# Residual add and RMS norm on one core: the fourth group's store issued between the second and third group's loads

## The chip, the core and the metric

The kernel runs on one core of a Trainium2 chip. The core has several engines with instruction streams of their own. Four matter here: VectorE (DVE in the profile) and ScalarE (ACT) compute, SyncE (SP) does nothing but issue transfers, and the DMA engines, 16 of them, move data between the chip's main memory (DRAM) and the on-chip buffers. TensorE has no work in this kernel and GpSimd (POOL) next to none.

The metric is the device time of one execution in microseconds (us). Before the change the median of three timed runs is 4016.13 us, the lowest 4003.17 and the highest 4017.06.

## The reference

```python
def setup_inputs():
    batch, seq, dim = 32, 2048, 2048
    # x, residual: (batch, seq, dim) float32; gamma: ones(dim); eps: 1e-6

def reference(x, residual, gamma, eps):
    z = x + residual
    rms = np.sqrt(np.mean(z ** 2, axis=-1, keepdims=True) + eps)
    return (z / rms * gamma).astype(np.float32)
```

There are 65,536 rows of 2048 float32 values. Each row is read twice (once from `x`, once from `residual`) and written once, so that 3 x 536.87 MB cross between DRAM and the core. No row needs anything of another row.

## The kernel before

**Tiles.** The rows are cut into 65 tiles, numbered 0 to 64. A full tile has 128 partitions with 8 rows each (8.39 MB per array); tile 0 has 3 rows per partition and tile 64 has 5. Tile `i` lives in buffer `z[i % 2]`: `x` is loaded there, `residual` is added in place, the normalized result is written over it, and the store reads it from there. So there are two tiles' worth of `z`. The residuals go to `r_area`, 9 rows per partition, in which the next tile's residual overwrites what the present tile's additions have already read.

**Groups.** Transfers of `x` into `z` and of results out of `z` are cut by partition into `Q = 4` groups: group `q` is the partitions `q, q+4, q+8, ...`, 32 of them, with all their rows (`group`, L145). One group's transfer of a full tile is 2.10 MB. A store of group `q` counts up the semaphore `s_out[q]`; a load of any group counts up `x_in`. The residual of a tile is one transfer of 8.39 MB.

**Compute.** `dve_turn` (L210) waits until all four groups of `x` and the residual are there, adds in three pieces, and then scales in two halves, each after ScalarE has given the root of the mean square; the last instruction counts up `done`. `act_turn` (L258) squares and sums each row, and in the middle of tile `i`, once the second of the three additions is through, it issues the load of the residual of tile `i + 1` on its own DMA queue (L161, q10 in the profile).

**Transfers by SP.** After a short beginning SP runs `sp_turn(sp, i)` (L177) for `i` = 1 to 63. All its transfers go to one queue (q1). Turn `i` stores the results of tile `i - 1` and loads `x` of tile `i + 1` into the buffer that these stores empty, group by group. SP works strictly in program order, so a wait in front of one transfer holds back everything behind it:

1. it waits for `done` of tile `i - 1` (L184);
2. it issues the stores of groups 0, 1 and 2 (L186);
3. for groups 0, 1 and 2 it waits until that group's store has landed (`s_out[q]`, L181) and issues the load of that group (L182, reported under L149);
4. it issues the store of group 3 (L189);
5. it waits until that store has landed and issues the load of group 3 (L190).

Then comes turn `i + 1`. Behind the turns, `sync_program` stores tile 63 in two halves and tile 64 in three pieces (L175).

In the profile the stores of the groups are `out_dram<-z` of L170, the loads of `x` are `z<-in_x_dram` of L149, and the residual is `r_area<-in_residual_dram` of L161.

Of the kernel before, what the change touches and what calls it, by code (L numbers as in the profile page):

```python
# [9 lines left out]
def kernel(  # L10
# [32 lines left out]
    Q = 4  # L43
# [16 lines left out]
    def rows(t, i):  # L60
        k = sizes[i]
        return t[starts[i] : starts[i] + P * k, :].rearrange("(p r) m -> p r m", r=k)
# [82 lines left out]
    def group(q):  # L145
        return slice(q, P, Q)

    def load_x(sp, i, q):
        sp.dma_start(out=z[i % 2][group(q), : sizes[i], :], in_=rows(x_f, i)[group(q)]).then_inc(  # L149
            ev["x_in"][i % 2], U  # L150
        )
# [17 lines left out]
    def store(sp, i, q):  # L169
        sp.dma_start(out=rows(o_f, i)[group(q)], in_=z[i % 2][group(q), : sizes[i], :]).then_inc(  # L170
            s_out[q], U
        )
# [4 lines left out]
    def sp_turn(sp, i):  # L177


        def load(q):  # L180
            sp.wait_ge(s_out[q], i * U)  # L181
            load_x(sp, i + 1, q)  # L182

        Turn(i).wait(sp, "done", -1)  # L184
        for q in range(Q - 1):
            store(sp, i - 1, q)  # L186
        for q in range(Q - 1):
            load(q)
        store(sp, i - 1, Q - 1)  # L189
        load(Q - 1)  # L190


    def add(v, i, a, b):
# [92 lines left out]
    def sync_program(sp):  # L286
        whole_x(sp, 0)
        load_r(sp, Turn(0))

        sp.wait_ge(tail_ev["add"], 1)  # L290
        for q in range(4):
            sp.dma_start(  # L292
                out=stage[32 * q : 32 * q + 1],
                in_=gamma.partition_broadcast(1).rearrange("p (a b) -> p a b", a=16),
            ).then_inc(g_in, U)
        load_r(sp, Turn(1))
        whole_x(sp, 1)
        for i in range(1, last):
            sp_turn(sp, i)
        (a0, b0), (a1, b1) = halves(last - 1)  # L300
        sp.wait_ge(half, 1)
        store_rows(sp, last - 1, a0, b0)
        Turn(last).wait(sp, "done", -1)
        store_rows(sp, last - 1, a1, b1)
        for k, (a, b) in enumerate(tail):
            sp.wait_ge(tail_ev["done"], k + 1)
            store_rows(sp, last, a, b)
# [94 lines left out]
```

## Time and profile before

| what | value |
|---|---|
| median of the timed runs | 4016.13 us |
| the profiled execution's own time | 3982.87 us |
| its span, first to last instruction | 3981.1 us |
| VectorE busy | 2300.7 us (58%) |
| ScalarE busy | 1059.7 us (27%) |
| read from DRAM / written | 1073.77 MB / 536.87 MB |
| share of the 16 DMA engines' time, queue of SP (q1) | 65.9% |
| the same, queue of ScalarE (q10) | 30.5% |

The profile is one execution. Its page gives sums over the whole span; the timeline gives single instructions with their starts; the view by windows gives, for any stretch of the span, each engine's busy time, the mean busy share of the DMA engines and the rate at which they moved data. That view books a DMA packet whole to the moment at which it starts (a packet here is 64 KB on one of the 16 engines), so a short window can show a share over 1, and windows are best cut where a transfer begins. The start of an SP row is when SP issues a transfer; when the transfer has landed is seen from the instruction that waited for it.

### The profile page before, as it was taken

To read this page: it belongs to the slowest core of one execution; us is meant where nothing else is said; L and a number is where in the kernel's file an instruction comes from. 1 tells how busy PE (TensorE), PEld (TensorE's weight loads), DVE (VectorE), ACT (ScalarE), POOL (GpSimd) and SP (SyncE) were. 2 spreads that over 40 slices of the span, in tenths; PEclk is the share of its full clock that TensorE was granted. 3 is DMA by queue.
4 is the path that set the end of the run, shared out by engine and by line. 5 is a ranking of instruction groups with operands and counts; after the bars stand their busy time and mean duration, and the time that the engine had idled before them with its cause. 6 is when DMAs were issued, how large, how long until landed. Compare 5 with 4: busy or idle time off the path is not lost.

```text
span 3981.1 us, 4005 instructions
## 1 busy us (share of the span) xinstructions
DVE 2300.7 (58%) x842; ACT 1059.7 (27%) x1157; POOL 0.2 (0%) x4
## 2 busy tenths in 40 slices
DVE  5646556465564655646556465564655646556465
ACT  2313223132231322313223132231322313223132
POOL 0000000000000000000000000000000000000000
DMA  9999999999999999999999999999999999999999
GB/s 421 411 392 420 399 402 410 390 415 396 400 411 400 411 400 408 403 400 412 400 409 402 400 411 400 400 411 400 413 398 411 411 400 411 400 400 410 390 421 379
DMA packets 34694, 1610.73 MB, mean 405 GB/s; under 512 B 9280, under 2 KB 9344, under 8 KB 9344
## 3 DMA queue, kind: packets, MB, share of 16 engines
q1 hardware_dynamic: 25616, 1085.34, 65.9%
q10 hardware_dynamic: 9072, 525.34, 30.5%
q14 instruction: 6, 0.05, 0.0%
HBM read 1073.77 MB, written 536.87 MB: 405 GB/s over the span
## 4 chain that ended last, share of the span: by engine, by line
DMA 94%; SPq 3%; DVE 1%; issue 1%; another core or an unknown queue 1%; ACT 0%; ACTq 0%; DVEq 0%
DMA out_dram<-z 93%; SPq L170 2%; SPq L149 1%; DVE z L200 1%; DVE z L195 1%; DMA z<-in_gamma_dram 0%; DMA z<-in_x_dram 0%; ACT sq_junk L246 0%; SPq L292 0%; DVE z L311 0%; ACT rms L256 0%; DVE rstd L219 0%; ACTq L161 0%; DVE tail_rstd L329 0%
## 5 line engine op out<-in xcount | busy, mean ns | idle before, releaser
L195 DVE TENSOR_TENSOR z<-z,r_area 128x8192 f32<-128x8192 f32 (+2 forms) x192 | 1104.8, 5809 | 1589.9 <-DMA z<-in_x_dram 1579.0
L246 ACT ACTIVATE sq_junk<-z 128x2048 f32<-128x2048 f32 x512 | 962.1, 1879 | 2891.2 <-DVE z L195 2880.9
L200 DVE SCALAR_TENSOR_TENSOR z<-z,rstd,gamma_tile 128x2048 f32<-128x2048 f32 x507 | 1156.5, 2343 | 4.5
L246 ACT ACTIVATION_READ_ACCUMULATOR sq_junk<-z 128x1 f32 x512 | 95.4, 186 | 0.0
L219 DVE RECIPROCAL rstd<-rms 128x4 f32<-128x4 f32 (+1 forms) x128 | 22.3, 174 | 58.2 <-ACT rms L256 58.2
L256 ACT ACTIVATE rms<-ssq,eps_tile 128x4 f32<-128x4 f32 (+1 forms) x128 | 38.0, 297 | 11.7
L200 DVE SCALAR_TENSOR_TENSOR z<-z,tail_rstd,gamma_tile 128x2048 f32<-128x2048 f32 x5 | 11.6, 2346 | 0.1
L313 DVE LOAD_MASK_SELECT gamma_tile<-z x1 | 0.0, 14 | 16.3 <-DMA z<-in_gamma_dram 16.3
L195 DVE TENSOR_TENSOR z<-z 128x2048 f32<-128x2048 f32 x3 | 6.7, 2284 | 0.0
L313 DVE STREAM_SHUFFLE gamma_tile<-z 128x2048 f32<-128x2048 f32 x1 | 2.3, 2290 | 0.0
L311 DVE MEMSET z<- 128x2048 f32 x1 | 1.8, 1765 | 0.4 <-issue 0.4
L246 ACT ACT_TABLE_LOAD x1 | 1.3, 1283 | 0.9 <-SPq L80 0.9
L256 ACT ACT_TABLE_LOAD x1 | 1.3, 1283 | 0.1
L256 ACT ACTIVATE tail_rms<-tail_ssq,eps_tile 128x2 f32<-128x2 f32 (+1 forms) x3 | 0.9, 295 | 0.1
L310 DVE MEMSET eps_tile<- 128x1 f32 x1 | 0.1, 59 | 1.0 <-SPq L80 1.0
L329 DVE RECIPROCAL tail_rstd<-tail_rms 128x2 f32<-128x2 f32 (+1 forms) x3 | 0.5, 158 | 0.0
L383 POOL MEMSET const-bfloat16-1.0<- 128x1 bf16 x1 | 0.1, 101 | 0.0
L383 POOL MEMSET const-uint8-127<- 128x1 uint8 x1 | 0.1, 101 | 0.0
L383 POOL MEMSET const-float32-0.0<- 128x1 f32 x1 | 0.1, 98 | 0.2 <-issue 0.2
L383 POOL MEMSET const-float32-1.0<- 128x1 f32 x1 | 0.1, 98 | 0.0
## 6 DMA issues: line engine op xcount, KB each, us to landing
out_dram<-z SPq DMA_DIRECT2D x2, 4096.0 KB, 20.9
z<-in_x_dram SPq DMA_DIRECT2D x4, 1280.0 KB
r_area<-in_residual_dram ACTq DMA_DIRECT2D x1, 5120.0 KB, 25.6
out_dram<-z SPq DMA_DIRECT2D x2, 2048.0 KB, 8.6
z<-in_x_dram SPq DMA_DIRECT2D x249
out_dram<-z SPq DMA_DIRECT2D x248, 20.6
z<-in_x_dram SPq DMA_DIRECT2D x1, 3072.0 KB
z<-in_residual_dram SPq DMA_DIRECT2D x1, 3072.0 KB, 17.2
```

What stands on the lines that cost most here:

```text
L149: sp.dma_start(out=z[i % 2][group(q), : sizes[i], :], in_=rows(x_f, i)[group(q)]).then_inc(ev["x_in"][i % 2], U)
L170: sp.dma_start(out=rows(o_f, i)[group(q)], in_=z[i % 2][group(q), : sizes[i], :]).then_inc(s_out[q], U)
L195: return v.tensor_add(out=s, in0=s, in1=res(i, a, b))
L200: ins = v.scalar_tensor_tensor(out=s, in0=s, scalar=rs[:, c + g - a : c + g - a + 1], in1=gamma_tile[:, :], op0=mult, op1=mult,)
L219: v.reciprocal(out=rstd[p][h][:, :n], in_=rms[p][h][:, :n]).then_inc(dve, U)
L246: s.activation(out=sq_junk[:, :], in_=src[:, g, :], func=Act.Square, accum_out=sq[:, c + g - a : c + g - a + 1],)
L256: return s.activation(out=rm, in_=sq, func=Act.Sqrt, bias=eps_tile[:, :], scale=inv_d)
L310: v.memset(eps_tile[:, :], float(eps))
L311: v.memset(stage, 0.0).then_inc(tail_ev["add"], 1)
L313: v.stream_shuffle(gamma_tile[:, :].rearrange("p (a b) -> p a b", a=16), stage, [0] * 32)
L329: v.reciprocal(out=tail_rstd[:, a:b], in_=tail_rms[:, a:b]).then_inc(dve, U)
L383: nc = _bacc.Bacc("TRN2", target_bir_lowering=False, num_devices=1)
```

## The change

Only the order of SP's instructions within a turn changes. The store of group 3 is issued after the loads of groups 0 and 1, and before the load of group 2, where it was issued after the load of group 2. Nothing is added or removed: a turn still has four stores and four loads with the same sizes, the same waits stand in front of the same transfers, and no instruction of VectorE or ScalarE is touched. `load(q)` is the inner function of `sp_turn` that waits for `s_out[q]` and issues the load.

```diff
         for q in range(Q - 1):
             store(sp, i - 1, q)
-        for q in range(Q - 1):
+        load(0)
+        load(1)
+        store(sp, i - 1, Q - 1)
+        for q in range(2, Q):
             load(q)
-        store(sp, i - 1, Q - 1)
-        load(Q - 1)
```

SP's stream of a turn with full tiles before the change (turn 2 of 63; L170 is a store, L149 a load, each of one group; in brackets the semaphore that it waits for):

```order
L170 DMA out_dram<-z 32x16384 [waits done1]
L170 DMA out_dram<-z 32x16384 x2
L149 DMA z<-in_x_dram 32x16384 [waits s_out0]
L149 DMA z<-in_x_dram 32x16384 [waits s_out1]
L149 DMA z<-in_x_dram 32x16384 [waits s_out2]
L170 DMA out_dram<-z 32x16384
L149 DMA z<-in_x_dram 32x16384 [waits s_out3]
```

The same turn after the change:

```order
L170 DMA out_dram<-z 32x16384 [waits done1]
L170 DMA out_dram<-z 32x16384 x2
L149 DMA z<-in_x_dram 32x16384 [waits s_out0]
L149 DMA z<-in_x_dram 32x16384 [waits s_out1]
L170 DMA out_dram<-z 32x16384
L149 DMA z<-in_x_dram 32x16384 [waits s_out2]
L149 DMA z<-in_x_dram 32x16384 [waits s_out3]
```

The last store, which waits for nothing, has moved up by one load; between it and the load that waits for its landing there now stands the load of group 2, where nothing stood before.

SP's stream at the last turn (63, whose loads are those of the shorter tile 64) and the first store behind it, before the change:

```order
L149 DMA z<-in_x_dram 32x10240 [waits s_out1]
L149 DMA z<-in_x_dram 32x10240 [waits s_out2]
L170 DMA out_dram<-z 32x16384
L149 DMA z<-in_x_dram 32x10240 [waits s_out3]
L175 DMA out_dram<-z 128x8192 [waits half]
```

And after it:

```order
L149 DMA z<-in_x_dram 32x10240 [waits s_out1]
L170 DMA out_dram<-z 32x16384
L149 DMA z<-in_x_dram 32x10240 [waits s_out2]
L149 DMA z<-in_x_dram 32x10240 [waits s_out3]
L175 DMA out_dram<-z 128x8192 [waits half]
```

The same move is made there; the stores of the end stand where they stood.

## The prediction

> **What bounds the kernel now.** I begin with the page: the span, the engines, and the DMA rows.
>
> ```profile
> span 3981.1 us, 4005 instructions
> DVE 2300.7 (58%) x842; ACT 1059.7 (27%) x1157; POOL 0.2 (0%) x4
> DMA  9999999999999999999999999999999999999999
> GB/s 421 411 392 420 399 402 410 390 415 396 400 411 400 411 400 408 403 400 412 400 409 402 400 411 400 400 411 400 413 398 411 411 400 411 400 400 410 390 421 379
> DMA packets 34694, 1610.73 MB, mean 405 GB/s; under 512 B 9280, under 2 KB 9344, under 8 KB 9344
> ```
>
> No compute engine is near its limit, and the DMA engines are over nine tenths busy in every slice: the transfers set the time. A slice of about 100 us hides what happens within a turn, though. So I ask who waits, first all engines, then SP's queue:
>
> ```profile
> DVE z L195 <- DMA z<-in_x_dram: 1579.0, 63, 26.1
> DVE z L195 <- DMA r_area<-in_residual_dram: 11.0, 1, 11.0
> ```
>
> ```profile
> SPq L149 <- DMA out_dram<-z: 3612.7, 252, 38.2
> ```
>
> VectorE waits some 25 us for `x` in each turn, so neither it nor ScalarE sets the pace; for the residual it waited once. SP spends nearly the whole span waiting for stores to land before it may load. Such a wait costs nothing while the DMA queues hold other work. Whether they do is seen in one turn from the middle, SP's rows (the three loads of L149 from narrow windows), with the residual's issue and VectorE's first addition and last scaling of a tile:
>
> ```profile
> 1964.23 0.47 SPq L149 DMA_DIRECT2D z<-in_x_dram  x1
> 1964.74 1.87 SPq L170 DMA_DIRECT2D out_dram<-z  x3
> 1973.06 8.69 DVE L195 TENSOR_TENSOR z<-z,r_area 128x8192 f32<-128x8192 f32 x1 [25.00 <-DMA z<-in_x_dram]
> 1977.79 0.51 SPq L149 DMA_DIRECT2D z<-in_x_dram  x1
> 1982.63 0.51 SPq L149 DMA_DIRECT2D z<-in_x_dram  x1
> 1987.65 0.47 SPq L149 DMA_DIRECT2D z<-in_x_dram  x1
> 1988.16 0.60 SPq L170 DMA_DIRECT2D out_dram<-z  x1
> 1988.40 0.34 ACTq L161 DMA_DIRECT2D r_area<-in_residual_dram  x1
> 2005.33 4.60 DVE L200 SCALAR_TENSOR_TENSOR z<-z,rstd,gamma_tile 128x2048 f32<-128x2048 f32 x2
> 2026.19 0.47 SPq L149 DMA_DIRECT2D z<-in_x_dram  x1
> ```
>
> I call the loads L0 to L3 and the stores S0 to S3, by group. The first row is L3 of a turn; behind it S0, S1, S2 of the next turn are issued at once. L0, L1 and L2 follow as S0, S1 and S2 land, 4.84 and 5.02 us apart. S3 and the residual go out at 1988.2 to 1988.4. Then SP stands still for 38 us until S3 has landed at 2026.19, and only then issues the next L3. The next stores, whose data VectorE had ready at 2005.33 + 4.60 = 2009.93, stand in SP's program behind that L3. So at 2026.19, with S3 landed, what else is in the queues? Windows over the DMA engines, cut at these points, say nothing:
>
> ```profile
> 1972.05:1986.55 14.50, 13.49 (x2) 4.70 (x5) 0.00 (x0) 1.00 1.00 434
> 1986.55:2025.45 38.90, 22.39 (x12) 11.81 (x14) 0.00 (x0) 1.00 1.00 431
> 2025.45:2027.40 1.95, 0.00 (x0) 0.00 (x0) 0.00 (x0) 1.00 0.00 0
> 2027.40:2034.05 6.65, 0.00 (x0) 0.00 (x0) 0.00 (x0) 1.00 1.06 345
> 1965.45:2027.40 61.95, 35.88 (x13) 16.51 (x18) 0.00 (x0) 1.00 0.97 406
> ```
>
> The last two numbers of a row are the DMA share and the rate. While S0 to S2 run (first row) and while L0 to L2, S3 and the residual run (second), the engines are full: 434 and 431 GB/s. Then the residual and S3 end together, both queues are **drained**, and for 1.95 us no packet starts. L3, alone behind the hole, moves its 2.10 MB in 6.65 us, where 2.10 MB at 434 GB/s take 4.83. The whole turn takes 61.95 us for 4 + 4 + 4 times 2.10 MB = 25.17 MB; at 434 GB/s that is 57.99. **The hole and the slow restart together cost 61.95 - 57.99 = 3.96 us a turn**; 1.95 of it is the hole, 2.0 the rest.
>
> **The change part by part.** No instruction, byte or wait is added or removed, and no VectorE or ScalarE row moves. Three things move on SP's queue.
>
> *S3 is issued earlier.* It goes out behind L1, at about the 1982.6 of the rows above instead of 1988.16, past L2 and its wait for S2. S3 itself waits for nothing, its data being finished long before. In the queue it takes the third place, behind L0 and L1, instead of the fourth.
>
> *L2 stays where it was in time.* It still waits for S2's landing (1987.65 above), and issuing S3 in front of it costs the 0.60 us of its row at a moment when SP waits anyway. Ahead of it S2, L0, L1 and S3 fill the queue, so SP is not late; were that cover gone, it would be 0.6 us a turn, 37 us in all.
>
> *L3's wait for S3 is now covered.* After S2's landing the queue of SP holds L0, L1, S3, L2 and ScalarE's holds the residual: the same 16.8 MB as before, but the last in SP's queue is now L2, not S3. When S3 lands, all of L2 (4.83 us at 434 GB/s) and whatever is left of the residual are still to be moved. The way from S3's end to L3's first packet showed as the 1.95 us hole. So L3 arrives at least 4.83 - 1.95 = 2.9 us before the engines run dry, and more if the residual has not ended. Right behind L3 SP issues the next S0 to S2 without a wait: the tile's `done` comes 2009.93 - 1973.06 = 36.87 us after its `x` has landed, and a turn is 58 at the least, so these stores have over 20 us to spare. The hole does not move elsewhere: during S0 to S2 the next load is issued as each one lands, with at least one more store in the queue, as the first window shows already.
>
> What is late next? Nothing up to the DMA rate itself. VectorE's chain of 36.87 us is far under 58. The residual is issued 1988.40 - 1973.06 = 15.34 us after the tile's `x` landed. Its time to land is the same in every turn that I asked for (spans 100 to 3900):
>
> ```profile
> DMA to landing us min/median/max: 37.7/37.9/38.6
> ```
>
> 15.34 + 37.9 = 53.2 us, inside 58.
>
> How often? The hole needs a turn that is drained. These are the first L3 of that kind, the last, and the windows on them, with the L3 of turn 1 ahead of them:
>
> ```profile
> 90.85 0.47 SPq L149 DMA_DIRECT2D z<-in_x_dram  x1
> 158.82 0.47 SPq L149 DMA_DIRECT2D z<-in_x_dram  x1
> 3941.19 0.47 SPq L149 DMA_DIRECT2D z<-in_x_dram  x1
> ```
>
> ```profile
> 158.50:160.00 1.50, 0.00 (x0) 0.00 (x0) 0.00 (x0) 1.00 0.00 0
> 3940.90:3942.40 1.50, 0.00 (x0) 0.00 (x0) 0.00 (x0) 1.00 0.00 0
> ```
>
> Turn 1 (90.85) lies in the warm-up, where the residual's load still runs (VectorE's single wait for it, 11.0 us). Turns 2 to 63 are 62, and (3941.19 - 158.82) / 61 = 62.0 us a turn confirms the count. The saving is 62 x 3.96 = 245.5 us. At the end nothing changes but the start: VectorE's work on tile 64 and the last stores hang on its `x` as before.
>
> **Sum.** 3982.87 (the profiled execution's own time) - 245.5 = 3737.4 us. The median of the runs shown lies 4016.13 - 3982.87 = 33.3 us above the profiled run, from a cause that the profile doesn't show; I leave that distance in: **3771 us**. As a cross-check, 1610.73 MB at 434 GB/s are 3711 us; the 26 us on top are the beginning, the end, and warm-up.
>
> The size that the trace doesn't show is L3's pace when it starts with the engines full. From one side, it runs as S0 to S2 do (4.83 us); from the other, its slowness (6.65) is its own and only the 1.95 us hole goes: 62 x 1.95 = 121 us. I take the first, since L0, also a load, follows S2 in the second window, where 431 GB/s leave no room for such a delay. Both ends are kept for the range.
>
> At this place the Trainium skill has a rule on the price: "DMA: Bandwidth & Descriptors", Anatomy of one DMA, gives each transfer about 2.0 us fixed (fitted on the other way of issuing, by GpSimd), mostly the confirmation of the last byte. By it the covered round trip would be worth 62 x 2.0 = 124 us and the time about 3892; the hole's 1.95 us agrees, while the 6.65 us of L3 speak for more.
>
> **The rivals.**
>
> *Only the hole goes.* As worked out: 3982.87 - 121 + 33.3 = 3895 us. For it: L3's slow part comes after the hole. Against: no other load shows it.
>
> *The engines can't hold 434 for long.* The fullest slice of the page has 421 GB/s. At that rate throughout, 1610.73 MB take 3826 us; with the 33.3 and a few us of beginning, 3861. Against: that slice contains the beginning of the kernel, and the 38.90 us stretch ran at 431 with reads and writes mixed. On this the skill's "HBM Reference", Specifications (TRN2), has a rule: a core streaming alone gets about 425 GB/s, bounded by its DMA engines. By it 1610.73 MB take 3790 us, with 33.3 and the beginning about 3826; the windows here show more, so far over stretches of 39 us.
>
> *The change doesn't do what it says: no change, 4016 us.* If the empty 1.95 us were not the drained queue but a pause that the engines take between a turn's end and L3 whatever lies behind, the turn would stay at 62. Against: the hole sits exactly on SP's round trip, and no packets are queued then.
>
> *Slower: the residual becomes the late one.* It enters at 15.34 us into the tile, with L0, L1, S3 and L2 in SP's queue. If the engines served it only behind these (4 x 4.83 = 19.3 us) and then shared with L3 and the next stores packet by packet (2 x 19.3 us), it would land 58 us after its issue, and VectorE would start a tile every 15.34 + 58 = 73.3 us: 62 x (73.3 - 62.0) = 701 us more, 4717. It decides as soon as the residual takes over 62.0 - 15.34 = 46.7 us to land. Against: it lands in 37.9 now with as many transfers queued ahead or beside it.
>
> **How the numbers follow.** Forecast (hole and slow restart gone) 0.69; rate below 434 GB/s 0.10; only the hole 0.08; no change 0.08; residual late 0.05. The prediction is the likeliest, 3771. Downwards the floor is the profiled run's 3737 without the 33.3; a little under it the range begins, 3730. Upwards it takes in the rate and the hole cases, 3900. That leaves out no change and slower, 0.13, and a little at the edges. A measurement of this kernel tells about 0.5% from no change, some 20 us; the first three cases are faster by far more: 0.87 faster, 0.08 within it, 0.05 slower.
>
> **What would show it.** After the change a turn's L3 should be issued several us before the DMA engines have finished L2 and the residual, no window of 1.5 us at L3 should be empty, a turn should take about 58.0 us between equal rows of SP, L0 to L2 should still follow the landings of S0 to S2, VectorE's wait for `x` should shrink by about 4 us a turn, and the mean rate should be near 431 GB/s. A hole elsewhere, VectorE waiting for the residual in most turns, or L3 taking over 6 us with full queues would make the prediction wrong.

## The result and the profile after

| | before | after |
|---|---|---|
| median of the timed runs, us | 4010.93 (4 runs, 4003.17 to 4017.06) | 3740.54 (4 runs, 3735.12 to 3749.47) |
| the profiled execution's own time, us | 3982.87 | 3735.12 |
| mean rate over the span, GB/s | 405 | 431 |

The ratio of after to before is 0.9329, with a 95% interval of 0.9302 to 0.9356. The sum made against the profiled execution had given 3737.4 us; the profiled run after has 3735.12. The forecast for the median, 3771, lies 30 us too high, and that is taken up below.

The page of the changed kernel, its span, DMA rows and queues (packets, MB, share of the 16 engines' span):

```profile
span 3733.3 us, 4005 instructions
...
DMA  9999999999999999999999999999999999999999
GB/s 415 436 428 437 437 428 436 428 436 428 435 431 435 433 434 431 436 431 434 436 429 437 435 432 434 433 433 433 433 433 432 433 428 436 428 437 433 430 433 392
DMA packets 34694, 1610.73 MB, mean 431 GB/s; under 512 B 9280, under 2 KB 9344, under 8 KB 9344
## 3 DMA queue, kind: packets, MB, share of 16 engines
q1 hardware_dynamic: 25616, 1085.34, 67.4%
q10 hardware_dynamic: 9072, 525.34, 32.6%
```

The two shares add up to 100.0%; before they were 65.9 + 30.5 = 96.4%. The page shows no idle time of the DMA engines any more, and all slices but the first and the last lie between 428 and 437 GB/s, where they had lain around 405.

SP's rows of one turn from the middle (the lines of the file have moved by one behind the change, so L196 is the former L195):

```profile
1954.02 0.47 SPq L149 DMA_DIRECT2D z<-in_x_dram  x1
1970.98 0.51 SPq L149 DMA_DIRECT2D z<-in_x_dram  x1
1975.83 0.51 SPq L149 DMA_DIRECT2D z<-in_x_dram  x1
1976.38 0.68 SPq L170 DMA_DIRECT2D out_dram<-z  x1
1980.69 0.47 SPq L149 DMA_DIRECT2D z<-in_x_dram  x1
2012.09 0.47 SPq L149 DMA_DIRECT2D z<-in_x_dram  x1
2024.36 8.69 DVE L196 TENSOR_TENSOR z<-z,r_area 128x8192 f32<-128x8192 f32 x1 [21.22 <-DMA z<-in_x_dram]
```

These are L3, then L0 and L1 behind the landings of S0 and S1, S3 at once behind L1, L2 behind S2's landing, and L3 of the next turn. From L3 to L3 it is 58.07 us, where it was 61.96. S3 lands by 2012.09, and L3, issued then, is through when VectorE starts at 2024.36, 12.27 us later. Its 2.10 MB take 4.83 us at 434 GB/s, so by this estimate the engines still had some 7 us of other work when it was issued. Two windows over this turn, the first inside the stretch of S0 to S2, the second the whole turn:

```profile
1960.00:1974.50 14.50, 8.23 (x1) 0.00 (x0) 0.00 (x0) 1.00 1.00 434
...
1954.00:2012.10 58.10, 35.88 (x13) 16.53 (x18) 0.00 (x0) 1.00 1.00 433
```

The stretch of stores runs at the 434 GB/s that it had before; now the whole turn does (433, share 1.00). VectorE's waits, over all turns:

```profile
DVE z L196 <- DMA z<-in_x_dram: 1308.7, 62, 22.4
...
DVE z L196 <- DMA r_area<-in_residual_dram: 33.3, 2, 17.1
```

VectorE waits for its input (1579.0 + 11.0) - (1308.7 + 33.3) = 248.0 us less. That is the whole gain of the span, 3981.1 - 3733.3 = 247.8 us.

The shares also say of what the gain consists. Before, the DMA engines were idle for 3.6% of 3981.1 us, that is 143 us, and busy for 3838; now they are busy for all 3733 with the same bytes. So 143 us were idle time, 2.3 us for each of the 62 turns, and the other 105 us, 1.7 a turn, were packets that took longer.

### The profile page after: what moved, and what is told of

Read it like the earlier page. It is cut to its first block, busy times and chain, and to the rows that moved or that the text cites. A ratio compares the mean times of both kernels' runs of the same rounds, so it can differ in the third digit from the quotient of the medians.

```text
span 3733.3 us, 4005 instructions
## 1 busy us (share of the span) xinstructions
DVE 2300.7 (62%) x842; ACT 1060.9 (28%) x1157; POOL 0.2 (0%) x4
## 4 chain that ended last, share of the span: by engine, by line
DMA 92%; SPq 4%; DVE 2%; issue 1%; another core or an unknown queue 1%; ACT 0%; ACTq 0%; DVEq 0%
DMA out_dram<-z 90%; SPq L170 3%; SPq L149 2%; DVE z L196 1%; DMA r_area<-in_residual_dram 1%; DVE z L201 1%; DMA z<-in_gamma_dram 0%; DMA z<-in_x_dram 0%; ACT sq_junk L247 0%; SPq L293 0%; DVE z L312 0%; ACT rms L257 0%; DVE rstd L220 0%; ACTq L161 0%
## 5 line engine op out<-in xcount | busy, mean ns | idle before, releaser
L196 DVE TENSOR_TENSOR z<-z,r_area 128x8192 f32<-128x8192 f32 (+2 forms) x192 | 1104.8, 5810 | 1342.0 <-DMA z<-in_x_dram 1308.7
L196 DVE TENSOR_TENSOR z<-z 128x2048 f32<-128x2048 f32 x3 | 6.7, 2284 | 0.0
## 6 DMA issues: line engine op xcount, KB each, us to landing
out_dram<-z SPq DMA_DIRECT2D x248, 21.5
```

What stands on the lines that cost most here:

```text
L196: return v.tensor_add(out=s, in0=s, in1=res(i, a, b))
```

## The experiments

The theory: the time came from the drained queues at each turn's end, and anything that stands in a queue while SP learns that S3 has landed removes it. The rivals: the early place of S3 or the mixing of stores and loads is what helps, or the hole alone (121 us) and not what the prediction calls the slow restart. Each experiment below ran beside the kernel before on the same chip; in the first four that has a median of 4002.39 us (19 runs), in the last four 4002.49 (9 runs). They are called e1 to e8 in the order in which they stand; the last section holds e7 and e8.

### The kernel before, again

No edit.

> The kernel before, once more, for its scatter: its profiled run lay 33 us under the median of its timed runs, while the changed kernel's profiled run lies 5 us under its median. Theory A (the distance sits in the hole at the end of each turn: the round trip from S3's landing to L3's first packet, and L3's restart, vary from run to run): about 4000 to 4017 us, and a profile of a slower run shows 62.0 plus up to 0.5 us a turn, with the difference in the hole or in L3, while the stretch with full queues still runs at 431 to 434 GB/s. Theory B (a difference between chips or runs that touches everything): the full-queue stretch itself is slower by 0.8%, about 427 to 430 GB/s.

Measured: 4003.65 us median of 10 runs, 3997.74 to 4008.96; ratio 0.9999 (0.9989 to 1.0008). Its profiled run was one of the slower ones. Its page, the queues, and windows over one turn (S0 to S2; L0 to L2, S3 and the residual; a stretch around L3's issue in which no packet starts; L3), and under them the like stretch in the first profile of this kernel:

```profile
span 4006.5 us, 4005 instructions
...
q1 hardware_dynamic: 25616, 1085.34, 65.5%
q10 hardware_dynamic: 9072, 525.34, 30.5%
```

```profile
1982.50:1997.00 14.50, 13.30 (x2) 4.51 (x5) 0.00 (x0) 1.00 1.00 434
1997.00:2035.70 38.70, 22.57 (x12) 11.99 (x14) 0.00 (x0) 1.00 1.00 434
2034.50:2038.30 3.80, 0.00 (x0) 0.00 (x0) 0.00 (x0) 1.00 0.00 0
2038.30:2045.00 6.70, 0.00 (x0) 0.00 (x0) 0.00 (x0) 1.00 1.00 313
```

```profile
2023.55:2027.35 3.80, 0.00 (x0) 0.00 (x0) 0.00 (x0) 1.00 0.00 0
```

The stretches with full queues are not slower, so theory B falls: S0 to S2 run at 434 GB/s in both profiles, and the second stretch moves the same 16.8 MB at a share of 1.00 (the prediction's 431 for it comes from a window that ends 0.2 us further in the stretch without starts). The engines were busy 96.0% of 4006.5 us, that is 3846 us, against 3838 in the first profile: of the 25.4 us more, about 17 are idle time and 8 longer packets (each share is rounded to 0.1%, 4 us). All 38 runs of this kernel in the experiments lie between 3996 and 4010 us, above the 3982.87 of the profile that the prediction was read from; why that one run was faster isn't shown. Theory A holds for most of the distance, but not by a longer hole: in both turns shown no packet starts for 3.80 us. The packet records of the two traces from 150 to 3650 us say where the idle time is. No engine has a packet for 1.6 us a turn in both, but an engine is idle for 2.4 us a turn on average in the first and 2.7 in the second, so in the second the engines run dry further apart from each other.

The same rows correct the reading of the hole. A packet takes 2.42 us where the queues are full (14.50 us for six of them on each engine), so of the 3.80 us without a start the first 2.4 are still covered by packets that run. The prediction's 1.95 us began 1.9 us into this stretch, and its start was chosen, not measured. L3 behind the hole has a share of 1.00 over 6.70 us for two packets on each engine: the engines are busy, with packets of 3.35 us.

### All four stores ahead of the loads

Against the changed kernel:

```diff
-        for q in range(Q - 1):
+        for q in range(Q):
             store(sp, i - 1, q)
-        load(0)
-        load(1)
-        store(sp, i - 1, Q - 1)
-        for q in range(2, Q):
+        for q in range(Q):
             load(q)
```

> All four stores of a turn ahead of its loads: S0 S1 S2 S3, then L0 to L3. Theory (only that something stands in the queue behind S3 when it lands): the same as the changed kernel, 3735 to 3750 us, no hole, about 58.1 us a turn; a better covered round trip brings nothing more. Rival (the place between the loads matters, since stores and loads mix better there): slower than the changed kernel by tens of us, 3770 or more, with the full-queue rate under 431 GB/s. Rival (the earlier the store, the better): faster than 3735.

Measured: 3732.47 us median of 4 runs (3732.05 to 3732.95), ratio 0.9318 (0.9303 to 0.9334), which overlaps with that of the changed kernel. The page's two queues add up to 99.9%. The place between the loads is not what helps: with no load between the stores it is as fast. The median lies just under the theory's 3735, where the last rival had put it. Whether this order is a little faster was left to a run of both on one chip, below.

### S3 where it was, L3 behind the next turn's S0

Against the kernel before:

```diff
-        def load(q):
+        def load(q, i=i):
...
         Turn(i).wait(sp, "done", -1)
-        for q in range(Q - 1):
+        store(sp, i - 1, 0)
+        if i > 1:
+            load(Q - 1, i - 1)
+        for q in range(1, Q - 1):
             store(sp, i - 1, q)
         for q in range(Q - 1):
             load(q)
         store(sp, i - 1, Q - 1)
-        load(Q - 1)
+        if i == last - 1:
+            load(Q - 1)
```

> S3 is left where it was before the change, behind L2; instead L3 and its wait for S3 are moved behind the first store S0 of the next turn, so that S0 stands in the queue when S3 lands. Theory (any cover does): no hole, 58 to 58.5 us a turn, 3740 to 3765 us; VectorE waits less for x since x lands about 5 us later. Rival (S3's early place is what brings the time): about 4010 us as before.

Measured: 3756.48 us median of 4 runs (3754.18 to 3757.49), ratio 0.9377 (0.9362 to 0.9393). S3 stands behind L2 as before the change, and 246 of the 4002.39 us go all the same. So it is not S3's early place; a store that covers the wait for S3 removes the holes as well. This is the clearest of the runs on that question, since it shares with the changed kernel nothing but the cover. The page's queues are full, as they are after the change:

```profile
q1 hardware_dynamic: 25616, 1085.34, 67.5%
q10 hardware_dynamic: 9072, 525.34, 32.4%
```

The span is 3754.8 us, 21.5 longer than that of the changed kernel, at 99.9% busy: that difference is mostly packets that took longer, and why is open.

### The changed order, and the drained queue put back

Against the changed kernel, a wait for the landing of L0 to L2 in front of L3:

```diff
-        for q in range(2, Q):
-            load(q)
+        load(2)
+        sp.wait_ge(ev["x_in"][(i + 1) % 2], ((i + 1) // 2) * Q * U + (Q - 1) * U)
+        load(3)
```

> The changed kernel with its order, and one wait more: SP issues L3 only when L0 to L2 have landed. S3 keeps its early place; only the emptied queue comes back. Theory (the hole is the cost): an empty window of about 2 us ahead of each L3, L3 in about 6.7 us, 62 us a turn, 3980 to 4010 us. Rival (the order brings the time, the empty queue does not matter): 3740 to 3760 us.

Measured: 4011.79 us median of 10 runs, ratio 1.0021 (1.0011 to 1.0031): the whole gain is gone, and 9 us more. Its L3, VectorE's start on that tile, and a window ahead of L3's first packet:

```profile
2035.27 0.47 SPq L149 DMA_DIRECT2D z<-in_x_dram  x1
2044.34 8.69 DVE L197 TENSOR_TENSOR z<-z,r_area 128x8192 f32<-128x8192 f32 x1 [26.05 <-DMA z<-in_x_dram]
```

```profile
2032.60:2036.40 3.80, 0.00 (x0) 0.00 (x0) 0.00 (x0) 1.00 0.00 0
```

The hole is back, again 3.80 us without a packet's start, and L3 takes 9.07 us from issue to VectorE's start, as the 8.91 us (2026.19 to 2035.10) did in the kernel before. With e3 this settles the point from both sides: without the order and with the cover the time is gained, with the order and without the cover it is lost.

### A hole between L3 and S0

Against the changed kernel, SP waits for all of `x` of the tile in work ahead of S0:

```diff
         Turn(i).wait(sp, "done", -1)
+        Turn(i).wait(sp, "x_in")
         for q in range(Q - 1):
```

> The changed kernel, and before S0 of each turn SP waits until all of x of the tile in work has landed (L3 is then the last transfer out, both queues are empty). The emptied queue now lies between L3 and S0 instead of between S3 and L3, so the first transfers behind it are three stores, issued together, in place of one load. Theory A (the cost is the round trip plus a slow restart of whatever comes first): a hole of about 2 us and a restart of about 2 us a turn, 62 us, 3980 to 4010 us. Theory B (the slow 6.65 us is peculiar to a load that runs alone with nothing behind it or to reads from DRAM): only the hole of about 2 us, 60 us a turn, 3855 to 3885 us. If neither hole nor slowness costs anything: 3740.

Measured: 3980.61 us median of 4 runs (3978.99 to 3982.72), ratio 0.9946 (0.9931 to 0.9962). In total it is theory A's number, though 22 us (0.5%) under the kernel before. One turn by windows: the hole; 12.15 us of stores; 3 us at the end of S2; the rest; 3 us from the middle of the rest; the next hole; the turn from hole to hole:

```profile
1970.60:1972.05 1.45, 0.69 (x1) 0.00 (x0) 0.00 (x0) 1.00 0.00 0
1972.05:1984.20 12.15, 12.15 (x2) 4.05 (x5) 0.00 (x0) 1.00 1.00 432
1984.20:1987.20 3.00, 3.00 (x2) 2.01 (x3) 0.00 (x0) 1.00 1.06 350
1987.20:2029.60 42.40, 20.03 (x11) 10.44 (x12) 0.00 (x0) 1.00 1.01 427
2007.00:2010.05 3.05, 1.22 (x1) 0.00 (x0) 0.00 (x0) 1.00 1.08 344
2032.65:2034.05 1.40, 0.73 (x1) 0.00 (x0) 0.00 (x0) 1.00 0.00 0
1972.05:2034.10 62.05, 35.96 (x14) 16.50 (x18) 0.00 (x0) 1.00 0.97 406
```

The turn is 62.05 us, as long as with the hole at its old place, but theory A's wording is wrong: the stores behind this hole run at 432 GB/s from the start. The slow part comes later, in two rounds of one packet on each engine, 350 GB/s at 1984.20 and 344 at 2007.00. By the bytes the first is still the end of S2: 12.15 us at 432 GB/s are 5.25 of the 6.29 MB of S0 to S2. The second comes 35 us behind the hole, with work in both queues. So a drained queue costs about 4 us in both places tried, about half of it in packets that take longer; these are neither bound to a load nor to the start behind the hole, so that a slow *restart* isn't shown. What makes them longer stays open.

### Only the residual as cover

Against the changed kernel, L2 waits for S3 as well:

```diff
         store(sp, i - 1, Q - 1)
+        sp.wait_ge(s_out[3], i * U)
         for q in range(2, Q):
             load(q)
```

> The changed kernel, with L2 waiting for S3's landing as well as for S2's. SP's queue is then empty when S3 lands, and only the residual on ScalarE's queue can cover the round trip. Counted from the changed kernel's turn, S3 lands when some two of the residual's eight 1.05 MB pieces are still to come (5 us). Theory (any queue's work covers, about 2 us suffice): no hole, 58 to 59 us a turn, 3740 to 3790 us. Rival (SP's own queue has to hold the cover): a hole of 2 us a turn or more, 3860 to 4010 us.

Measured: 3815.75 us median of 4 runs (3802.05 to 3830.32), ratio 0.9537 (0.951 to 0.9564), between the two theories. SP's own queue is empty when S3 lands, and yet 187 of the 4002.49 us are gained, so the other queue's work does cover. It is not enough in every turn: after the first turns VectorE starts successive tiles 57.9 to 62.9 us apart. The page's queues:

```profile
span 3809.9 us, 4068 instructions
...
q1 hardware_dynamic: 25616, 1085.34, 67.1%
q10 hardware_dynamic: 9072, 525.34, 32.0%
```

The engines are 99.1% busy, which leaves 34 us idle; the rest of the distance to the changed kernel is longer packets. The expected 5 us of residual left over was counted from one turn of the changed kernel, and the turns here differ.

### The changed kernel and the stores-first one on one chip

The two kernels as they are above, with no further edit.

> The changed kernel again, on the same chip as the next one, to compare the two: 3735 to 3750 us.

> All four stores ahead of the loads, beside the changed kernel on the same chip. Theory (both have the round trip covered; what is left is the DMA rate): equal to it within 0.3%, that is 3730 to 3750. If a longer cover still brings something: faster by 8 us or so, as between the runs of the two so far (3732.5 and 3740.5).

Measured: the changed kernel 3745.43 us (5 runs, 3730.18 to 3753.35), ratio 0.9344 (0.9325 to 0.9363); stores first 3732.50 us (5 runs, 3731.92 to 3732.84), ratio 0.9324 (0.9312 to 0.9337). The changed kernel's best run, 3730.18, is the fastest of all, but its runs scatter over 23 us and those of the other over 1 us. The profile taken of the changed kernel here, one of 3753.35 us, shows where the time goes:

```profile
GB/s 413 436 433 433 430 433 433 433 432 435 433 433 427 431 435 433 436 435 431 432 435 436 435 433 430 434 435 436 426 432 416 427 421 427 423 427 426 426 428 384
```

From the thirty-first slice on it runs at 416 to 428 GB/s instead of mostly 430 to 436, with the shares of both queues still adding to 100.0%. So the queues stay full and the packets take longer. Why the stretch begins is open. In the median stores first is 13 us (0.3%) faster here, and eight of the nine runs of the changed kernel lie above all nine of stores first; but the two ratios' intervals overlap, so that what is clear is its smaller scatter. Neither expectation is settled: hardly any idle time is left in either (99.9 and 100.0% busy), and the difference lies in how long packets take.

## Why the prediction was right, and where it was off

**The bound and the hole.** Right. The DMA engines set the time, at 434 GB/s while their queues are full, and the order of SP's instructions drained them once a turn. The changed order with the hole put back (the run that waits for L0 to L2, e4) is as slow as before.

**S3 earlier, L2 in place, L3 covered.** Right, row by row: S3 goes out behind L1 (1976.38), L2 still follows S2's landing, and L3 is issued by estimate some 7 us before the engines would have run dry, where at least 2.9 was worked out. Nothing else came late: the residual lands in 37.8 us in the median of turns from 300 to 3600 us of the span, as before:

```profile
DMA to landing us min/median/max: 36.4/37.8/38.8
```

**The size per turn.** 57.99 us was forecast, 58.07 measured in the turn shown. The choice between its two ends, the hole alone (121 us) or hole and slowness (245.5), was right: 247.8 us went. The split was less sound. The 1.95 us of the hole hung on where the window was cut (no packet starts for 3.80 us, and for 2.42 of them a packet is still running); by the shares the idle time is 2.3 us a turn and the rest 1.7. And the rest need not be a slow restart: with the hole ahead of S0 (e5) the stores behind it run at 432 GB/s, and the longer packets come later. The fixed 2.0 us a transfer of the Trainium skill ("DMA: Bandwidth & Descriptors", Anatomy of one DMA) would have given 124 us, and the runs show twice that per drained queue. The 425 GB/s for a core streaming alone of the Trainium skill ("HBM Reference", Specifications (TRN2)) is exceeded a little: 431 over the span, 433 over a whole turn.

**The 33.3 us carried over.** This term was wrong, and it makes up the error of the forecast. It was left in as a distance "from a cause that the profile doesn't show". The second profile of the kernel before (e1), 25.4 us longer than the first, shows some 17 of them as idle time of drained engines, which the change removes, while the full stretches are as fast in both. Without it the sum gives 3737.4 us, and 3740.54 was measured. Seen from the medians, the gain is 4010.93 - 3740.54 = 270.4 us, or 4.36 for each of the 62 drained turns, where the profile at hand showed 3.96.

**The rivals.** *Only the hole goes* (3895) and *the rate can't be held* (3861) both fall with the 433 GB/s over a whole turn. *No change* falls with the result. *The residual late* did not come, but VectorE waited for it twice instead of once, for 33.3 us in all, both in the first turns:

```profile
111.21 17.36 DVE L196 TENSOR_TENSOR z<-z,r_area 128x8192 f32<-128x8192 f32 x3 [16.20 <-DMA r_area<-in_residual_dram]
165.17 17.36 DVE L196 TENSOR_TENSOR z<-z,r_area 128x8192 f32<-128x8192 f32 x3 [17.08 <-DMA r_area<-in_residual_dram]
```

Both lie in the page's second slice (93 to 187 us), in which the engines moved 436 GB/s, so that they cost nothing there.

## What to carry to other kernels

Where the DMA engines bound a kernel, look at one turn for the moment at which an issuing engine waits for the last transfer that it has out: the busy share of a long slice (here 96%) hides it. In this kernel it was enough that some other ready transfer of 2.10 MB stood in the queue there, and its place in the order mattered little: a cover in each of three places brought 246 to 270 us, and one by the other queue that did not reach in every turn 187. And where a profiled run lies beside the median of the timed ones, ask whether the distance belongs to what the change removes before it is carried over.

## What the runs showed that was not expected

SP's issue of S0 to S2, 1.87 us for three before the change, now takes much longer in some turns. The three stores behind L3 in the turn shown, the first and then the other two:

```profile
1954.53 1.63 SPq L170 DMA_DIRECT2D out_dram<-z  x1
...
1956.20 4.47 SPq L170 DMA_DIRECT2D out_dram<-z  x2
```

That is 6.1 us, with L2, L3 and part of the residual still out; what lengthens an issue isn't shown. It cost nothing here, since S0 needs only to be there when L3 ends. Not understood are the longer packets behind a hole (e5) and the changed kernel's stretches at 416 to 428 GB/s with full queues (e7), of which the times of nine stores-first runs, 3731.92 to 3732.95, show no sign.
